# Attention of the first two chunks issued among the later chunks' k, q, v, g products, with buffers of its own

## The chip, the cores and the metric

One core of one Trainium2 chip runs the kernel. The metric is device time in microseconds, the median of several executions. Matrix work is in fp32r with every operand split into a high and a low part, so one product of fp32 quality is three matmuls.

## What is computed

A decoder trunk of two layers over 2048 positions of width 1024, and a last norm. Layer 0 is a gated short convolution. Layer 1 is stick-breaking attention with 8 heads of 64. Cut to what matters here:

```python
h = rmsnorm(x, norm_a)
b, c, xin, g = split(h @ w_in_a, 4)
x = x + ((b * conv3(c * xin)) * silu(g)) @ w_out_a
k, v = split(rmsnorm(x, norm_kv) @ w_kv, 2)
q, g = split(rmsnorm(x, norm_b) @ w_in_b, 2)
...
z = q @ k.T / 8                       # per head, keys before the query only
rev = reverse_cumsum(log_sigmoid(-z))
o = exp(z + rev) @ v
...
x = x + (o * silu(g)) @ w_out_b
return rmsnorm(x, norm_f)
```

## The kernel before, in words

Positions lie reversed along the free axis (a host layout), in four chunks of 512 columns; features lie on the 128 partitions. The two layers' products are made with a fast scheme of seven block products for two chunks at once, chunks (0, 1) and then (2, 3): `fast_unit` (line 848) forms a unit, seven products of 12 matmuls each of 128x128 by 128x512 (84 matmuls), into three PSUM banks named fa, fd and fe. `fast_operands` (742) forms the operands b11, t1, t2, b22, t3, b21, t4 of a pair from its rows, and `operand` (682) gives each a place among the tags that the `HOMES` table names.

The weights of a unit are seven sums and differences of blocks, each split into high and low. `fast_weights` (804) either loads them from DRAM, where an earlier call put them, or loads four raw blocks (`raw_blocks`, 795, which multiplies by the norm's gain on GpSimd), forms the seven on VectorE (`combine`, 781), splits them, uses them, and stores them to DRAM for the next pair. Two of the eight k, q, v, g units are prepared ahead (`prepare_pair`, 845; `READY` is 0 and 4).

After the mixer's output products (`po` parts) come the k and q units (`pair_kq`, 992, parts kq00 to kq03 for chunks 0 and 1, kq20 to kq23 for chunks 2 and 3) and the v and gate units (`pair_vg`, 1002). They store split k (four DMAs of 64 partitions for each pair of heads and chunk), split q, the differences of neighbouring v rows, and silu(g) to DRAM. Each unit forms two chunks, so all of chunks 0 and 1 is in DRAM when the first four units of each sort are done.

`attend` (1030) is the attention of one chunk and one head. It looks only at the query's own 128-block and the one before it; what that leaves over is gathered in a tile `left`, and if any of it isn't zero a full version runs at the end (it isn't entered with these inputs). It loads q2 (two DMAs of 64 partitions), kt and vv, each with two buffers. Eight z matmuls give the logits, ScalarE makes R by a sigmoid, GpSimd masks (`affine_select`), VectorE runs four scans, GpSimd copies `left`; seven or eight transposes (wt) bring the blocks the other way, ScalarE and VectorE split them into wth and wtl, and av matmuls multiply them with vv; two operations put the head's half into the tile ot. `gate_kept` (1240) adds the first v row, multiplies by the gate, both on GpSimd, and splits the result into the og operands. There are 32 heads, parts a00 to a37, and gates g00 to g32.

The output product (`out_kept`, 1256, parts o0 to o2; `out_b_last` and `finish` for chunk 3) takes og and the output weights wob, which `keep_ob` (1234) loads for good into eight tiles of the `act` tag; these tiles are free only when the operands of the products are done with. `fold_gains` (914) has split those weights and put them into DRAM. `norm_kept` (1268) ends chunks 0 to 2.

What sets the order: all operations are recorded first. `PLAN` (36) gives each part a start and an end, a key is laid over the part's operations, and `Recorder.order` (285) picks one operation after another by a list schedule: the one that can start first by its own costs of engines, buffers in turn, and DMA (`DMA_RATE`, 70), and the lower key among equals. The order in which each engine issues is then fixed. An engine does its queue strictly in order, and SyncE (SP) issues all the DMAs of this part, so a load that waits for a buffer holds up all the loads and stores behind it. Buffers of one tag are given in turn.

Every recorded operation is emitted from line 358, so the profile's rows all have that line and are told apart by tile names.

Of the kernel before, what the change touches and what calls it, by code (L numbers as in the profile page):

```python
# [10 lines left out]
F32 = mybir.dt.float32  # L11
F32R = mybir.dt.float32r
# [4 lines left out]
P = 128  # L17
# [10 lines left out]
FIRST = (("act", [2, CH], NA), ("R", [CH], NR), ("q2", [2, CH], 2), ("kt", [CH], 2), ("vv", [CH], 2), ("wth", [CH], NWTS),  # L28
# [41 lines left out]
DMA_RATE, DMA_BEFORE, DMA_AFTER, FLY = 0.36, 1.0, 2.8, 8  # L70
# [296 lines left out]
def kernel(  # L367
# [56 lines left out]
    k_all = [dram.tile([P, S], F32, name=f"k_d_{h}") for h in range(NH)]  # L424
    k_d = [[k_all[h][:, cols(c)] for h in range(NH)] for c in range(NCH)]
# [121 lines left out]
    def norm_x_late(c, between=None):  # L547

        hc, xs = [], []
        for k in range(KD):  # L550
            if between is not None:
                between(k)
            tag, bufs = (("og", KD), ("ld", NL) if k < NL else ("vv", 2) if k == NL else ("ot", 2))[c]
            x = sb.tile([P, CH], F32, name=f"xh_{c}_{k}", tag=tag, bufs=bufs)
            nc.sync.dma_start(out=x, in_=xT[k * P:(k + 1) * P, cols(c)])
            xs.append(x)
            ga = gains["a"][:, k:k + 1]
            hk = act_tile(f"h_{c}", k)
# [123 lines left out]
    def operand(c, nm, k, raw, eng=nc.vector):  # L682

        if k == 0:
            fast_b[c, nm] = []
            other = {"t1": "t4", "t4": "t1"} if isinstance(c, tuple) and c[0] == "kq" else {}
            home[nm] = list(HOMES[other.get(nm, nm)])
        tag = home[nm].pop(0)
        if tag in ("act", "q2"):
            t = sb.tile([P, 2, CH], F32R, name=f"op_{nm}_{c}_{k}", tag=tag, bufs=BUFS[tag])  # L690
            pair = (t[:, 0, :], t[:, 1, :])
        else:
            tags = [tag, home[nm].pop(0)]
# [48 lines left out]
    def fast_operands(key, load, eng, hold=False):  # L742
# [11 lines left out]
        for k in range(Q):  # L754
            b.append(raw("b12", 0, k, *((("ot", 2) if k < 2 else ("p", 2)) if hold else ())))
            eng.tensor_sub(a[k], b[k], a[k])
            operand(key, "t1", k, a[k])
# [7 lines left out]
        for k in range(Q):  # L765
            if not hold:
                b[k] = raw("c12", 0, k, "ot", 2)
            eng.tensor_sub(b[k], d[k], b[k])
# [223 lines left out]
    def pair_kq(c0, i):  # L992
        for c, (k, q) in enumerate(pair_unit(c0, i, f"kq{i}"), c0):
            hl = halves(f"khl_{c}_{i}_", k)
            for j in range(2):
                for m in range(2):
                    nc.sync.dma_start(out=k_d[c][2 * i + j][m * 64:(m + 1) * 64, :], in_=hl[m][j * 64:(j + 1) * 64, :])
# [32 lines left out]
    def attend(c, h, ot):  # L1030
# [3 lines left out]
        q2 = sb.tile([P, 2, CH], F32R, name=f"q2_{nm}", tag="q2", bufs=2)  # L1034
        for i in range(2):
            nc.sync.dma_start(out=q2[i * 64:(i + 1) * 64, :, :].bitcast(F32), in_=q_d[c][hb][hi_ * 64:(hi_ + 1) * 64, :, :])
        kt = sb.tile([P, CH + P], F32R, name=f"kt_{nm}", tag="kt", bufs=2)
        vt = sb.tile([P, 5, 2, 64], F32R, name=f"vv_{nm}", tag="vv", bufs=2)
        n = 5 if c else 4
        at = 4 * (NCH - 1 - c)  # L1040
        nc.sync.dma_start(out=kt[:, 0:n * P].bitcast(F32), in_=k_all[h][:, at * P:(at + n) * P])
# [4 lines left out]
        for i in range(2):  # L1046
# [8 lines left out]
            r = sb.tile([P, CH], F32, name=f"R_{nm}_{i}", tag="R", bufs=NR)  # L1055
# [18 lines left out]
        for i, places in enumerate((((1, 0), (1, 1), (2, 1), (2, 2)), ((3, 2), (3, 3), (0, 0), (4, 3)))):  # L1074
# [6 lines left out]
            wh = sb.tile([P, CH], F32R, name=f"wth_{nm}_{i}", tag="wth", bufs=NWTS)  # L1081
            wl = sb.tile([P, CH], F32R, name=f"wtl_{nm}_{i}", tag="wtl", bufs=NWTS)
# [15 lines left out]
    def attention(c, h, ot):  # L1098
# [4 lines left out]
        for i in range(2):  # L1103
            nc.scalar.dma_start(out=q2[i * 64:(i + 1) * 64, :, :].bitcast(F32), in_=q_d[c][hb][hi_ * 64:(hi_ + 1) * 64, :, :])
# [135 lines left out]
    def gate_kept(c, k, ot):  # L1240
# [3 lines left out]
        nc.gpsimd.tensor_mul(ot, ot, sg)  # L1244
        og = act_tile(f"og_{c}", k)
        og_t.setdefault(c, []).append(og)
        split(og[:, 0, :], og[:, 1, :], ot)
# [123 lines left out]
    part("fl", any_left)  # L1371
    for c in range(3):
# [10 lines left out]
    with tc.If(some != 0, preferred_fallthrough_block=False):  # L1383
        og_t.clear()
        acc_b.clear()
        for c in range(NCH):
            for hb in range(NH // 2):
                ot = sb.tile([P, CH], F32, name=f"all_ot_{c}_{hb}", tag="ot", bufs=2)
# [32 lines left out]
```

## Time and profile before

| | |
|---|---|
| median of 3 runs | 1430.42 us (1422.63 to 1435.01) |
| the profiled execution's own time | 1427.81 us |
| its span, first to last instruction | 1425.8 us |
| mean granted TensorE clock | 0.976 |
| moved by DMA | 409.31 MB, 287 GB/s |
| last product unit's matmuls end | about 1175 us |
| attention's z matmuls | 954.6 to 1343.7 us |
| output products (pob) | 1188.4 to 1392.1 us |

How to read the rows that follow: a row of a stretch gives its bounds, its length, then busy time and number of instructions for PE (matmul), PEld (weight load), DVE (VectorE), ACT (ScalarE) and POOL (GpSimd), then the granted clock, the busy share of the 16 DMA engines and GB/s. A row of a group gives the engine, the operation, out<-in by tile names, the shape and the count, then the busy time and the mean of one in ns, then the idle time of the engine before them and what ended it. A row of the chain gives its start, its length and what it was. Matmuls are pipelined, so the mean of one is longer than the step from one to the next. A row of a DMA gives the count, the size and the median time from issue to landing.

### The profile page before, as it was taken

What the parts mean: (1) busy time and instruction counts of PE and PEld (TensorE: products, weight loads), DVE (VectorE), ACT (ScalarE), POOL (GpSimd) and SP (SyncE); (2) the same over time, 40 slices, a digit from 0 to 9 for tenths busy, and PEclk for the clock granted to TensorE, in tenths of its full rate; (3) what the DMA queues carried; (4) which work ended last, traced back from release to release, by engine and by line L of the source; (5) the groups of instructions that cost most, each with busy time, mean ns of one, the idle gap of its engine ahead of it and who ended that gap; (6) DMA issues with size and microseconds to landing.
All of it is one profiled execution on the core that took longest, in us unless ns stands there. A gap on an engine that the chain in (4) does not pass through costs nothing.

```text
span 1425.8 us, 18966 instructions
## 1 busy us (share of the span) xinstructions
PE 1330.1 (93%) x6174; PEld 1096.2 (77%) x6174; DVE 986.0 (69%) x1557; ACT 578.2 (41%) x999; POOL 389.5 (27%) x447
## 2 busy tenths in 40 slices
PE   7999999999999999999999999998899986787994
PEld 6787888888888888888887787776778775576883
DVE  6999787879867655566584886568632387777864
ACT  6344443335333322233332444443422255455542
POOL 6252000000200001001216532242100135466775
PEclk9999999999999999999999999998999998999996
DMA  9648998688988999979997889995899999988433
GB/s 296 214 149 264 336 322 290 230 284 284 371 320 284 344 381 347 371 271 371 334 361 289 284 264 336 349 379 174 280 319 325 312 300 300 282 242 220 154 128 121
DMA packets 216413, 409.31 MB, mean 287 GB/s; under 512 B 20208, under 2 KB 89840, under 8 KB 216304
## 3 DMA queue, kind: packets, MB, share of 16 engines
q1 hardware_dynamic: 215104, 407.97, 85.4%
q8 instruction: 51, 0.84, 0.2%
q14 instruction: 58, 0.48, 0.1%
q0 software_dynamic: 160, 0.02, 0.1%
q10 hardware_dynamic: 1040, 0.00, 0.0%
HBM read 238.06 MB, written 169.87 MB: 286 GB/s over the span
## 4 chain that ended last, share of the span: by engine, by line
PE 70%; DMA 12%; DVE 11%; issue 3%; ACT 2%; POOL 1%; SPq 0%; DVEq 0%; ACTq 0%; POOLq 0%
PE fa_B L358 11%; PE fa_C L358 10%; PE fa_o L358 6%; PE fd_B L358 5%; PE fd_C L358 5%; PE fa_vg L358 5%; PE fa_kq L358 5%; PE pob L358 4%; DMA kt<-k_d 4%; DMA q<-q_d 3%; PE fd_o L358 3%; PE fe_B L358 3%; PE fe_C L358 2%; PE fd_vg L358 2%; PE fd_kq L358 2%
## 5 line engine op out<-in xcount | busy, mean ns | idle before, releaser
L358 POOL COPY halo<-p 128x2 f32<-128x2 f32 x32 | 17.3, 539 | 395.1 <-DVE p L358 394.6
L358 POOL TENSOR_TENSOR acc_x<-acc_x,sq_x 128x512 f32<-128x512 f32 x52 | 76.0, 1461 | 124.2 <-ACT sq_x L358 123.4
L358 DVE TENSOR_TENSOR_SCAN R<-R,ones 128x256 f32<-128x256 f32 x128 | 97.2, 798 | 7.4 <-POOL R L358 7.3
L358 PE MATMUL pob<-og,wob 128*128 128x512 f32 x360 | 98.6, 407 | 0.2 <-DVE og L358 0.2
L358 PE MATMUL fa_C<-op_t,whl_s_C 128*128 128x512 f32 x336 | 85.5, 390 | 0.6 <-DVE op_t L358 0.6
L358 PE MATMUL fa_B<-op_t,whl_s_B 128*128 128x512 f32 x336 | 83.1, 389 | 0.0
L358 PEld LDWEIGHTS pob<-og,wob 128*128 128x128 f32 x360 | 64.6, 191 | 11.5 <-DVE x L358 0.6
L358 PEld LDWEIGHTS fa_C<-op_t,whl_s_C 128*128 128x128 f32 x336 | 62.7, 188 | 13.9 <-DVE op_t L358 1.0
L358 PEld LDWEIGHTS fa_B<-op_t,whl_s_B 128*128 128x128 f32 x336 | 63.1, 188 | 13.1
L358 PE MATMUL z<-kt,q 128*128 128x256 f32 x256 | 49.4, 326 | 23.7 <-DMA kt<-k_d 21.9
L358 ACT ACTIVATE sq_x<-x 128x512 f32<-128x512 f32 x55 | 34.6, 631 | 77.9 <-DVE x L358 74.8
L358 PEld LDWEIGHTS z<-kt,q 128*128 128x128 f32 x256 | 40.0, 216 | 28.3 <-issue 22.0
L358 PE MATMUL wt<-ident,R 128*128 128x128 f32 x248 | 49.4, 289 | 7.4 <-DVE R L358 5.3
L358 DVE TENSOR_TENSOR wtl<-wt,wth 128x512 fp32r<-128x512 f32 x64 | 41.7, 665 | 19.0 <-ACT wth L358 16.6
L358 DVE SCALAR_TENSOR_TENSOR cv<-p,cw,cv 128x512 f32<-128x512 f32 x64 | 49.6, 775 | 6.8 <-ACT cv L358 3.5
L358 ACT CAST wth<-wt 128x512 fp32r<-128x512 f32 x64 | 35.9, 574 | 41.1 <-PE wt L358 33.3
L358 POOL TENSOR_SCALAR_AFFINE_SELECT R<-R 128x256 f32<-128x256 f32 x64 | 36.5, 578 | 58.4 <-ACT R L358 57.8
L358 PE MATMUL av<-wth,vv 128*128 128x256 f32 (+1 forms) x152 | 39.6, 293 | 11.5 <-DMA vv<-v_d 6.0
L358 DVE TENSOR_TENSOR x<-x,fa_o 128x512 f32<-128x512 f32 x32 | 21.9, 686 | 38.9 <-PE fa_o L358 28.4
L358 ACT ACTIVATE R<-z 128x512 f32<-128x512 f32 x64 | 36.9, 601 | 26.2 <-PE z L358 25.8
L358 PE MATMUL fa_B<-op_t,whl_a_B 128*128 128x512 f32 x168 | 45.4, 390 | 0.0
L358 PE MATMUL fa_C<-op_b,whl_a_C 128*128 128x512 f32 x168 | 45.3, 390 | 0.0
(1012 smaller groups left out, 3709.1 us busy)
## 6 DMA issues: line engine op xcount, KB each, us to landing
sw_s_C<-whl_s_C SPq DMA_DIRECT2D x32, 512.0 KB, 3.9
sw_s_B<-whl_s_B SPq DMA_DIRECT2D x32, 512.0 KB, 4.3
whl_s_o<-sw_s_o SPq DMA_DIRECT2D x32, 512.0 KB, 5.7
q<-q_d SPq DMA_DIRECT2D x64, 256.0 KB, 7.9
sw_a_C<-whl_a_C SPq DMA_DIRECT2D x24, 512.0 KB, 4.2
sw_a_B<-whl_a_B SPq DMA_DIRECT2D x24, 512.0 KB, 3.6
whl_s_C<-sw_s_C SPq DMA_DIRECT2D x24, 512.0 KB, 5.5
whl_s_B<-sw_s_B SPq DMA_DIRECT2D x24, 512.0 KB, 6.0
```

The lines of the kernel that those rows point to most:

```text
L358: getattr(o.engine.engine, o.name)(*map(real, o.args), **{k: real(v) for k, v in o.kw.items()})
```

## The change

- The keys of the plan from xk0 on are new, those of po22, po23 and fold too: fold comes earlier, and the heads of chunks 0 and 1 (a00 to a17) lie among kq2 and vg2. `DMA_RATE` goes from 0.36 to 0.33.
- The heads of chunks 0 and 1 get other places: kta and vva, new tags of one buffer each, for kt and vv; q2 takes a tile of the weights' tag whl (8 buffers), R one of og (8), wth and wtl of acc (2). The tag ot (2 buffers) goes; what used it takes kta and vva.
- The gated outputs of chunks 0 and 1 go to DRAM and are loaded and split later, in new parts h0 and h1 (`load_og`).
- q2 is loaded by one DMA over 128 partitions, which repeats each source row, so two neighbouring partitions hold the same row; k is stored with its high and low part on alternate partitions, by two DMAs of 128 partitions for a pair of heads in place of four of 64.
- The weights of a k, q, v or g unit that wasn't prepared ahead are formed from the raw blocks for each pair of chunks. They are no longer stored to DRAM or loaded back; for the later pair their sums and differences run on GpSimd.
- In the k, q, v, g units the operands t1, t2 and t4 trade places: t1 gets the tiles of q2, kt and vv, t2 those of R, wth and wtl, t4 those of act.

```diff
+    "kq20": (938.809, 984.97), "vg20": (994.417, 1022.11),
+    "kq21": (1117.4, 1118.71), "vg21": (1025.39, 1044.52), "kq22": (1066.01, 1107.98), "vg22": (1121.85, 1133.59),
+    "kq23": (1121, 1126.72), "vg23": (1045.19, 1089.24), "wo": (1165.87, 1206.27), "a00": (967.407, 970.474),
...
-    k_all = [dram.tile([P, S], F32, name=f"k_d_{h}") for h in range(NH)]
+    k_all = [dram.tile([2 * P, S], F32, name=f"k_d_{i}") for i in range(NH // 2)]
...
-            other = {"t1": "t4", "t4": "t1"} if isinstance(c, tuple) and c[0] == "kq" else {}
+            other = {"t1": "t4", "t2": "t1", "t4": "t2"} if isinstance(c, tuple) and c[0] == "kq" else {}
...
     def fast_weights(c, nm, key, srcs=None, gain=None):
         w = {}
+        if gain is not None and key not in split_d:
+            def put(n, raw):
+                w[n] = w_tile(f"{n}_{nm}")
+                split(w[n][:, 0], w[n][:, 1], raw)
+
+            combine(raw_blocks(nm, srcs, gain), put, nc.gpsimd if c == ("kq", 2) else nc.vector)
+            return w
...
-            for j in range(2):
-                for m in range(2):
-                    nc.sync.dma_start(out=k_d[c][2 * i + j][m * 64:(m + 1) * 64, :], in_=hl[m][j * 64:(j + 1) * 64, :])
+            for m in range(2):
+                nc.sync.dma_start(out=k_all[i][m::2, cols(c)], in_=hl[m])
...
-        q2 = sb.tile([P, 2, CH], F32R, name=f"q2_{nm}", tag="q2", bufs=2)
-        for i in range(2):
-            nc.sync.dma_start(out=q2[i * 64:(i + 1) * 64, :, :].bitcast(F32), in_=q_d[c][hb][hi_ * 64:(hi_ + 1) * 64, :, :])
-        kt = sb.tile([P, CH + P], F32R, name=f"kt_{nm}", tag="kt", bufs=2)
-        vt = sb.tile([P, 5, 2, 64], F32R, name=f"vv_{nm}", tag="vv", bufs=2)
+        early = c < 2
+        qtag, ktag, vtag, rtag, wtags = (("whl", NWB), ("kta", 1), ("vva", 1), ("og", KD), (("acc", 2), ("acc", 2))) if early else (
+            ("q2", 2), ("kt", 2), ("vv", 2), ("R", NR), (("wth", NWTS), ("wtl", NWTS)))
...
+        q2 = sb.tile([P, 2, CH], F32R, name=f"q2_{nm}", **home(qtag))
+        nc.sync.dma_start(out=q2.bitcast(F32), in_=q_d[c][hb][hi_ * 64:(hi_ + 1) * 64].unsqueeze(1).to_broadcast([64, 2, 2, CH]))
+        kt = sb.tile([P, CH + P], F32R, name=f"kt_{nm}", **home(ktag))
+        vt = sb.tile([P, 5, 2, 64], F32R, name=f"vv_{nm}", **home(vtag))
...
         nc.gpsimd.tensor_mul(ot, ot, sg)
+        if c < 2:
+            nc.sync.dma_start(out=og_d[c][k], in_=ot)
+        else:
+            split_og(c, k, ot)
...
+    def load_og(c):
+        for k in range(4):
+            r = ld512(f"ogl_{c}_{k}")
+            nc.sync.dma_start(out=r, in_=og_d[c][k])
+            split_og(c, k, r)
...
+    for c in range(2):
+        part(f"h{c}", load_og, c)
```

More of the change, by code (lines that the diff above doesn't have):

```diff
@@ L27 @@
 READY = (0, 4)
-FIRST = (("act", [2, CH], NA), ("R", [CH], NR), ("q2", [2, CH], 2), ("kt", [CH], 2), ("vv", [CH], 2), ("wth", [CH], NWTS),
+FIRST = (("act", [2, CH], NA), ("R", [CH], NR), ("q2", [2, CH], 2), ("kt", [CH], 2), ("vv", [CH], 2), ("kta", [CH + P], 1), ("vva", [CH + P], 1), ("wth", [CH], NWTS),
          ("wtl", [CH], NWTS), ("wraw", [Q, P], NRAW), ("whl", [2, Q, P], NWB))
@@ L68 @@
 SEM = 0.11
-DMA_RATE, DMA_BEFORE, DMA_AFTER, FLY = 0.36, 1.0, 2.8, 8
+DMA_RATE, DMA_BEFORE, DMA_AFTER, FLY = 0.33, 1.0, 2.8, 8
 class Base:
@@ L423 @@
     x1_d = [[dram.tile([P, CH], F32, name=f"x1_d_{c}_{k}") for k in range(KD)] for c in range(NCH)]
-    k_all = [dram.tile([P, S], F32, name=f"k_d_{h}") for h in range(NH)]
-    k_d = [[k_all[h][:, cols(c)] for h in range(NH)] for c in range(NCH)]
+    k_all = [dram.tile([2 * P, S], F32, name=f"k_d_{i}") for i in range(NH // 2)]
+    k_d = [[k_all[h // 2][(h % 2) * P:(h % 2 + 1) * P, cols(c)] for h in range(NH)] for c in range(NCH)]
     q_d = [[dram.tile([P, 2, CH], F32, name=f"q_d_{c}_{h}") for h in range(NH // 2)] for c in range(NCH)]
@@ L552, in norm_x_late @@
                 between(k)
-            tag, bufs = (("og", KD), ("ld", NL) if k < NL else ("vv", 2) if k == NL else ("ot", 2))[c]
+            tag, bufs = (("og", KD), ("ld", NL) if k < NL else (("vv", 2), ("kta", 1), ("vva", 1))[k - NL])[c]
             x = sb.tile([P, CH], F32, name=f"xh_{c}_{k}", tag=tag, bufs=bufs)
@@ L754, in fast_operands @@
         for k in range(Q):
-            b.append(raw("b12", 0, k, *((("ot", 2) if k < 2 else ("p", 2)) if hold else ())))
+            b.append(raw("b12", 0, k, *((("kta", 1), ("vva", 1), ("p", 2), ("p", 2))[k] if hold else ())))
             eng.tensor_sub(a[k], b[k], a[k])
@@ L766, in fast_operands @@
             if not hold:
-                b[k] = raw("c12", 0, k, "ot", 2)
+                b[k] = raw("c12", 0, k, ("kta", "vva")[k % 2], 1)
             eng.tensor_sub(b[k], d[k], b[k])
@@ L1033, in attend, with home @@
         nm = f"{c}_{h}"
-        q2 = sb.tile([P, 2, CH], F32R, name=f"q2_{nm}", tag="q2", bufs=2)
-        for i in range(2):
-            nc.sync.dma_start(out=q2[i * 64:(i + 1) * 64, :, :].bitcast(F32), in_=q_d[c][hb][hi_ * 64:(hi_ + 1) * 64, :, :])
-        kt = sb.tile([P, CH + P], F32R, name=f"kt_{nm}", tag="kt", bufs=2)
-        vt = sb.tile([P, 5, 2, 64], F32R, name=f"vv_{nm}", tag="vv", bufs=2)
+        early = c < 2
+        qtag, ktag, vtag, rtag, wtags = (("whl", NWB), ("kta", 1), ("vva", 1), ("og", KD), (("acc", 2), ("acc", 2))) if early else (
+            ("q2", 2), ("kt", 2), ("vv", 2), ("R", NR), (("wth", NWTS), ("wtl", NWTS)))
+        def home(tag):
+            return {"tag": tag[0], "bufs": tag[1]}
+        q2 = sb.tile([P, 2, CH], F32R, name=f"q2_{nm}", **home(qtag))
+        nc.sync.dma_start(out=q2.bitcast(F32), in_=q_d[c][hb][hi_ * 64:(hi_ + 1) * 64].unsqueeze(1).to_broadcast([64, 2, 2, CH]))
+        kt = sb.tile([P, CH + P], F32R, name=f"kt_{nm}", **home(ktag))
+        vt = sb.tile([P, 5, 2, 64], F32R, name=f"vv_{nm}", **home(vtag))
         n = 5 if c else 4
         at = 4 * (NCH - 1 - c)
-        nc.sync.dma_start(out=kt[:, 0:n * P].bitcast(F32), in_=k_all[h][:, at * P:(at + n) * P])
+        nc.sync.dma_start(out=kt[:, 0:n * P].bitcast(F32), in_=k_all[hb][hi_ * P:(hi_ + 1) * P, at * P:(at + n) * P])
         nc.sync.dma_start(out=vt[:, 0:n].bitcast(F32), in_=v_all[h][:, at:at + n])
@@ L1054, in attend @@
                         nc.ops[-1].deps.add(nc.ops[-2])
[L1055 removed]
+            r = sb.tile([P, CH], F32, name=f"R_{nm}_{i}", **home(rtag))
             nc.scalar.activation(r, ps, AF.Sigmoid, scale=-0.125)
@@ L1080, in attend @@
                 nc.tensor.transpose(wt[:, j * P:(j + 1) * P], blk(kb, qi), ident)
-            wh = sb.tile([P, CH], F32R, name=f"wth_{nm}_{i}", tag="wth", bufs=NWTS)
-            wl = sb.tile([P, CH], F32R, name=f"wtl_{nm}_{i}", tag="wtl", bufs=NWTS)
+            wh = sb.tile([P, CH], F32R, name=f"wth_{nm}_{i}", **home(wtags[0]))
+            wl = sb.tile([P, CH], F32R, name=f"wtl_{nm}_{i}", **home(wtags[1]))
             split(wh[:, 0:n], wl[:, 0:n], wt[:, 0:n])
@@ L1102, in attention @@
         q2 = sb.tile([P, 2, CH], F32R, name=f"q2_{nm0}", tag="q2", bufs=2)
-        for i in range(2):
-            nc.scalar.dma_start(out=q2[i * 64:(i + 1) * 64, :, :].bitcast(F32), in_=q_d[c][hb][hi_ * 64:(hi_ + 1) * 64, :, :])
+        nc.scalar.dma_start(out=q2.bitcast(F32), in_=q_d[c][hb][hi_ * 64:(hi_ + 1) * 64].unsqueeze(1).to_broadcast([64, 2, 2, CH]))
         av = psum.tile([P, CH], F32, name=f"av_{nm0}", tag="av", bufs=NAV)
@@ L1244, in gate_kept, with split_og @@
         nc.gpsimd.tensor_mul(ot, ot, sg)
+        if c < 2:
+            nc.sync.dma_start(out=og_d[c][k], in_=ot)
+        else:
+            split_og(c, k, ot)
+    def split_og(c, k, r):
         og = act_tile(f"og_{c}", k)
         og_t.setdefault(c, []).append(og)
-        split(og[:, 0, :], og[:, 1, :], ot)
+        split(og[:, 0, :], og[:, 1, :], r)
+    def load_og(c):
[3 more added lines that the diff above has]
+            split_og(c, k, r)
     def x2_rows(c):
@@ L1387 @@
             for hb in range(NH // 2):
-                ot = sb.tile([P, CH], F32, name=f"all_ot_{c}_{hb}", tag="ot", bufs=2)
+                ot = sb.tile([P, CH], F32, name=f"all_ot_{c}_{hb}", tag="og", bufs=KD)
                 for h in (2 * hb, 2 * hb + 1):
```

53 rows, old and new, of the table PLAN are left out of this document.

## Prediction

> **What bounds the kernel now.** I read the page first, then the busy times of five stretches of the span, the chain that ended last, and the matmuls in order of time where one head of the attention already runs among products.
>
> ```profile
> span 1425.8 us, 18966 instructions
> ...
> PE 1330.1 (93%) x6174; PEld 1096.2 (77%) x6174; DVE 986.0 (69%) x1557; ACT 578.2 (41%) x999; POOL 389.5 (27%) x447
> ...
> GB/s 296 214 149 264 336 322 290 230 284 284 371 320 284 344 381 347 371 271 371 334 361 289 284 264 336 349 379 174 280 319 325 312 300 300 282 242 220 154 128 121
> ```
>
> TensorE is the bound of the whole: busy 93% of the span. What a stage loses is read from stretches: 790 to 1143 us are the k, q, v, g products, 1143 to 1312 most of the attention, 1312 to 1398 the rest of it with the output products, then the last norm.
>
> ```profile
> 790.00:960.00 170.00, 165.15 (x742) 134.07 (x740) 121.55 (x189) 77.81 (x138) 61.09 (x54) 1.00 0.95 327
> 960.00:1143.00 183.00, 168.79 (x747) 136.15 (x747) 87.90 (x125) 56.27 (x98) 23.26 (x37) 0.97 0.85 283
> 1143.00:1312.00 169.00, 128.12 (x787) 109.85 (x788) 130.22 (x209) 89.28 (x162) 87.00 (x137) 0.91 0.97 268
> 1312.00:1398.00 86.00, 84.33 (x444) 70.26 (x442) 68.56 (x112) 44.56 (x75) 65.90 (x62) 0.99 0.47 154
> 1398.00:1426.00 28.00, 7.04 (x32) 6.61 (x32) 9.29 (x20) 3.68 (x7) 10.05 (x8) 0.58 0.30 107
> 1143.00:1250.00 107.00, 79.46 (x479) 67.87 (x480) 83.70 (x129) 54.77 (x101) 47.97 (x84) 0.89 1.04 295
> ```
>
> The columns are PE, PEld, DVE, ACT, POOL busy with counts, granted clock, DMA share, GB/s. In the third row PE is idle 41 of 169 us, the clock falls to 0.91 and the DMA engines are busy 0.97 of the time (1.04 up to 1250 us, at only 295 GB/s; the page has slices at 371 and 379). The chain there is loads behind loads:
>
> ```profile
> 565.98 2.72 PE fa_C L358 x12
> ...
> 1206.99 10.22 DMA kt<-k_d
> 1218.57 9.09 DMA q<-q_d
> 1227.67 8.82 DMA q<-q_d
> 1236.51 9.73 DMA q<-q_d
> ```
>
> So the attention stage is set by its loads, all on SP's queue, and not by PE; in the product stage the same chain is PE alone, 12 matmuls in 2.72 us (0.227 each).
>
> **How much is lost.** The counts and the price of a small matmul:
>
> ```profile
> L358 PE MATMUL pob<-og,wob 128*128 128x512 f32 x360 | 98.6, 407 | 0.2 <-DVE og L358 0.2
> ...
> L358 PE MATMUL z<-kt,q 128*128 128x256 f32 x256 | 49.4, 326 | 23.7 <-DMA kt<-k_d 21.9
> ...
> L358 PE MATMUL wt<-ident,R 128*128 128x128 f32 x248 | 49.4, 289 | 7.4 <-DVE R L358 5.3
> ...
> L358 PE MATMUL av<-wth,vv 128*128 128x256 f32 (+1 forms) x152 | 39.6, 293 | 11.5 <-DMA vv<-v_d 6.0
> ```
>
> ```profile
> 954.63 1.12 PE L358 MATMUL z<-kt,q 128*128 128x256 f32 x8
> 955.58 0.63 PE L358 MATMUL fa_vg<-op_t_('kq', 0)_2_7452,whl_s_vg 128*128 128x512 f32 x2
> ...
> 976.47 0.28 PE L358 MATMUL av<-wth,vv 128*128 128x256 f32 x1
> ...
> 983.22 0.27 PE L358 MATMUL av<-wtl,vv 128*128 128x128 f32 x1
> ```
>
> Eight z take 0.95 us among products (954.63 to the next start), 0.12 each; I price all attention matmuls at that. From 790 to 1398 the four rows hold 2720 matmuls: 1344 of the products (16 units of 84, by the code) and 384 of the output (360 pob and, by the code, 24 in the last step) at 0.227 make 392 us; 808 of the attention (256 + 248 + 2 x 152) at 0.12 make 97; the other 184, short ones and the last mixer-output products, at an estimated 0.14, 26. That is 515 us of work in 608: 93 are lost. The third stretch holds some 617 attention matmuls, 110 of the output and 60 others (its 787, split by names): 74 + 25 + 12 = 111, so 58 are lost there. The fourth loses about 3. The other 32 are lost in the first two (353 us, 9%), of which 19 show as idle (4.9 + 14.2); the first alone idles 2.9%. The 28 us after 1398 stay.
>
> **The change, part by part.**
>
> Attention of chunks 0 and 1 (16 of 32 heads) goes among the later products. PE's work is the same; 16 heads are 48 us by the price above. What is left for the last stage is 16 heads (48), 384 output matmuls (87) and about 5 of sums: 140 us; the product part becomes 515 - 140 = 375. The product part's rate of loss has its ends in today's product rows: 2.9% (idle of 790 to 960, where weights are formed from raw as the later pair's now will be) and 9% (all of 790 to 1143). I take the middle, 6%: 375/0.94 = 399, 24 lost. For the last stage the ends are the fourth stretch (3 of 86, 3.5%) and the third (58 of 169, 34%). Half of the heads, spread over as much output work, are nearer to the fourth: I take 7%, 140/0.93 = 150.5, 10.5 lost. Together 34.5 in place of 93: **58.5 us less**.
>
> Loads, stores and SP's queue. Each head loads q, kt and vv:
>
> ```profile
> q<-q_d SPq DMA_DIRECT2D x64, 256.0 KB, 7.9
> ...
> kt<-k_d SPq DMA_DIRECT2D x24, 320.0 KB, 7.8
> vv<-v_d SPq DMA_DIRECT2D x24, 320.0 KB, 7.2
> ...
> sw_s_kq<-whl_s_kq SPq DMA_DIRECT2D x12, 512.0 KB, 5.1
> sw_s_vg<-whl_s_vg SPq DMA_DIRECT2D x12, 512.0 KB, 6.6
> ```
>
> 1.18 MB a head, 18.9 MB for 16, enter the product part. Out of it go the weight stores of six units (12 + 12 of these two rows and 18 more by the code, 42 of 0.52 MB, 22 MB) and 42 loads, for which 24 raw loads of 0.26 MB come: 15.7 MB less. 107 MB in 353 us now (327 x 170 + 283 x 183) become 107 + 19 - 38 + 6 (the fold of w_out_b, planned earlier) + 4 (gated outputs to DRAM and back) = 98 in 399: 246 GB/s, under all these rows. The last stage moves 18.9 + 4.2 (wob) + 8.4 (x) + 8 (out) + 2 = 42 MB in 150 us, 280 GB/s, which is no longer far below the 295 of the saturated row. q in one issue in place of two, and k stores halved, take 64 issues off SP.
>
> Single buffers. kta and vva have one buffer, so the next vva load waits on SP for the last av of the head before. Behind it in SP's queue stand raw weights and k, q, v stores, for which the product units wait. Today's one interleaved head spends 976.47 to 983.2 in av; with 7.2 to land, a head then takes at least 14 us, 16 heads 227. The first v is in DRAM at about 900 us (an estimate from the product order), the product part ends at 790 + 399 = 1189: 289 us, 18 a head. It fits with 4 us to spare, so I price it at nothing; the rival below is the other end.
>
> Weights formed anew: for six units of the later pair 42 casts on ACT, 42 subtractions on DVE, and on POOL 24 gains and 24 sums.
>
> ```profile
> L358 DVE TENSOR_TENSOR fr_a_vg<-fr_a_vg,fr_a_vg 128x512 f32<-128x512 f32 x12 | 10.3, 858 | 0.1
> ...
> L358 DVE TENSOR_TENSOR whl_s_kq<-fr_a_kq,whl_s_kq 128x512 fp32r<-128x512 f32 x12 | 9.8, 821 | 2.3 <-ACT whl_s_kq L358 2.3
> ...
> L358 DVE TENSOR_TENSOR fr_a_kq<-fr_a_kq,fr_a_kq 128x512 f32<-128x512 f32 x12 | 8.2, 686 | 0.0
> ...
> L358 ACT CAST whl_s_kq<-fr_a_kq 128x512 fp32r<-128x512 f32 x12 | 7.5, 624 | 10.3 <-DVE fr_a_kq L358 3.4 <-PE fa_kq L358 2.4 <-PE fd_kq L358 1.8
> ...
> L358 POOL TENSOR_TENSOR fr_a_kq<-fr_a_kq,g_kv 128x512 f32<-128x512 f32 x6 | 7.1, 1191 | 35.9 <-DMA fr_a_kq<-in_w_kv_dram 35.9
> ```
>
> ACT 42 x 0.62 = 26 us, DVE 42 x 0.82 = 34, POOL 24 x 1.19 = 29 and 24 sums, whose nearest POOL row is this one with two whole inputs:
>
> ```profile
> L358 POOL TENSOR_TENSOR acc_x<-acc_x,sq_x 128x512 f32<-128x512 f32 x52 | 76.0, 1461 | 124.2 <-ACT sq_x L358 123.4
> ...
> L358 DVE TENSOR_TENSOR_SCAN R<-R,ones 128x256 f32<-128x256 f32 x128 | 97.2, 798 | 7.4 <-POOL R L358 7.3
> ...
> L358 DVE TENSOR_TENSOR wtl<-wt,wth 128x512 fp32r<-128x512 f32 x64 | 41.7, 665 | 19.0 <-ACT wth L358 16.6
> ```
>
> 24 x 1.46 = 35. DVE also gets 16 heads of four scans, two wtl and one ot (0.68): 5.2 us, 83. So DVE in the product part is 121.6 + 87.9 + 34 + 83 = 327 of 399 us, 82%. Its first stretch now has 121.55 of 170, 71%, beside a PE that idles 2.9%. All this lies beside PE's 375; without that cover it would be a bound of its own, the second rival. POOL is at 84 + 64 + about 31 (selects, left) + about 20 (gates) = 199 of 399, not a bound.
>
> The gated outputs of chunks 0 and 1 go to DRAM and back (8 stores, 8 loads, 8 splits later): off the path while they are back before the wob loads have landed. Other homes of the operands t1, t2, t4 only choose what frees first at the end of the products; bounds 0 to 3 us either way, in the 7%.
>
> Sum: 1427.8 (this execution's own time, 2 us over its span) - 58.5 = 1369. The median, 1430.42, is 2.6 higher, inside the runs' spread of 12.
>
> **Rivals.**
>
> 1. Loads still pace the last stage: 42 MB at the third row's 268 GB/s are 157 us, and the 4.2 MB of wob stand before its first output product, 14 at 295: 171, 20 more, **1389**. For it: that row's share of 0.97. Against: half of the heads.
> 2. POOL holds DVE up. If each of the 48 new POOL operations (64 us) delays a DVE operation by its length, DVE has 391 of 399; at 93% use the part takes 420, 21 more, **1390**. For it: the same subtraction and sum on DVE take 686 to 858. Against: 0.17 us of growth is far from 1.2. The Trainium skill, SBUF — State Buffer, "Who interferes with whom", says that "a DVE instruction with two SBUF inputs contends with a GpSimd instruction that reads SBUF"; by that rule this rival would hold, and the row's growth agrees in sign, not in size.
> 3. The loads of a head come faster: q as one load over 128 partitions rather than two over 64 lets the last stage move at the 371 of the page's better slices (42 MB in 113 us, so PE alone sets it), and losses are the low ends, 11 + 5: **1351**, lower still if the product part idles less than today. The Trainium skill, same page, "Door 1: The DMA port swizzle", says that 64 partitions reach only half of the ports; no row here shows one load alone.
> 4. The other side: the single buffers make heads nearly serial. From its first z to its last av the interleaved head takes 28.6 us (954.6 to 983.2); if kt can't be loaded under the head before, a period is 7.8 + 14 and some 2 of queueing, 24 us: 384 in a room of 289, and PE, in order, stands before a late z, 95 us: **1464**. It decides from 18 us a head; at 21.7 nothing is gained, at 22.8 it is slower by 1%. For it: today, with two buffers, z waits 21.9 us on kt. Against: kta is free after eight z, long before av.
> 5. The order puts the heads behind the products after all, so that the same loads stand at the end: **1425**. Against: the plan's numbers for chunks 0 and 1 lie among those of kq2 and vg2.
>
> **Chances.** 0.55 for the forecast (1350 to 1390), 0.1 each for rivals 1, 2 and 3, 0.08 for 4, 0.07 for 5. A measurement of this kernel can tell about 1% from no change (under 1416, over 1445). Faster 0.86, the same 0.07, slower 0.07. The range takes in rivals 1 to 3, product losses of 9% and a last stage at 20% (35): gain 21, 1407; below, rival 3 with 15 to spare: 1336 to 1408.
>
> **What would show it.** Right: z and av from about 910 us on; under 10 us of PE idle per 170 us until the products end near 1190; the stretch from there to the last output matmul 150 us, with the clock above 0.95; DMA share under 0.9 before 1190; no sw_s_kq or sw_s_vg stores. Wrong: PE waiting on kta or vva more than 4 us a head, DVE above 90% there, or a last stage over 170 us.

## The result and the profile after

| | before | after |
|---|---|---|
| median in the runs side by side | 1432.2 us (1422.63 to 1435.01) | 1383.73 us (1383.31 to 1384.27) |
| ratio | | 0.9673, 95% interval 0.9627 to 0.972 |
| the profiled execution's own time | 1427.81 us | 1383.76 us |
| last matmul of the mixer's output products (fa_o) starts | 805.5 us | 826.4 us |
| last matmul of the product units (fe_vg) starts | 1174.9 us | 1202.2 us |
| last output matmul (pol) starts | 1397.5 us | 1354.2 us |

The change is faster by 3.3%. The time lies inside the predicted range (1336 to 1408) and 14.7 us above the point forecast of 1369. First the head of the page after: span, busy times of the engines, traffic.

```profile
span 1381.8 us, 18877 instructions
...
PE 1321.8 (96%) x6174; PEld 1085.6 (79%) x6174; DVE 1028.7 (74%) x1599; ACT 596.3 (43%) x1041; POOL 450.4 (33%) x495
...
DMA packets 218268, 375.74 MB, mean 272 GB/s; under 512 B 18480, under 2 KB 100400, under 8 KB 218160
```

As many matmuls as before, 44 us less span, and 33.6 MB less traffic (409.31 before). The stretches of after, with the columns of the stretches in the prediction: two in the mixer, three in the product part, then what comes behind it, split in two.

```profile
300.00:350.00 50.00, 43.49 (x185) 35.30 (x184) 43.31 (x71) 23.82 (x42) 2.83 (x4) 0.93 0.80 276
650.00:820.00 170.00, 162.57 (x702) 130.94 (x701) 113.61 (x182) 55.69 (x95) 54.92 (x39) 0.98 0.95 335
820.00:960.00 140.00, 139.23 (x647) 114.95 (x646) 111.44 (x180) 68.80 (x123) 40.68 (x45) 1.00 0.69 233
960.00:1045.00 85.00, 79.81 (x387) 64.65 (x387) 80.39 (x105) 46.76 (x84) 45.77 (x52) 1.00 0.76 260
1045.00:1180.00 135.00, 134.36 (x701) 110.99 (x699) 109.89 (x147) 68.67 (x125) 90.29 (x103) 1.00 0.69 222
1180.00:1300.00 120.00, 113.99 (x670) 96.80 (x669) 97.46 (x156) 71.55 (x126) 76.70 (x96) 0.97 0.90 309
1300.00:1354.00 54.00, 53.19 (x279) 43.03 (x278) 40.95 (x80) 25.43 (x44) 43.54 (x42) 1.00 0.45 151
```

From 820 to 1180 us PE idles 6.6 us in 360 and the DMA engines are busy 0.69 to 0.76 of the time; before, the attention stretch alone idled 41 of 169 at 0.97. What follows, 1180 to 1354, idles 6.8 of 174. The first two rows are the other side. The same stretches in the kernel before, the second one up to the end of its mixer:

```profile
300.00:350.00 50.00, 50.00 (x222) 41.11 (x220) 44.93 (x73) 23.94 (x41) 1.55 (x4) 1.00 0.85 278
650.00:805.00 155.00, 151.77 (x672) 124.75 (x671) 94.93 (x158) 49.67 (x85) 53.06 (x39) 0.99 0.93 333
```

So something was lost before the products begin, for which the prediction's sum has no term. The longest waits of PE in the whole span of after (the longest, 6.7 us at the kernel's start, is as before and is left out), and the place of the first of them in the order of time, on PE and on DVE:

```profile
PE fa_B L359 <- DVE whl_s_B L359: 6.0, 1, 6.0
PE pst_x L359 <- DVE acc_x L359: 3.4, 1, 3.4
PE fa_o L359 <- ACT op_t_('o', 2)_2_6683 L359: 3.2, 1, 3.2
```

```profile
340.00 3.94 PE L359 MATMUL fa_B<-op_t,whl_s_B 128*128 128x512 f32 x10 [5.96 <-DVE whl_s_B L359]
```

```profile
333.05 0.70 DVE L359 TENSOR_TENSOR whl_s_B<-fr_a_B,whl_s_B 128x512 fp32r<-128x512 f32 x1
333.65 0.69 DVE L359 TENSOR_TENSOR xc<-xb,xc 128x512 f32<-128x512 f32 x1
334.25 0.70 DVE L359 TENSOR_TENSOR xb<-xb,xb 128x512 f32<-128x512 f32 x1
334.85 2.08 DVE L359 SCALAR_TENSOR_TENSOR xb<-xb,g_a,rs 128x512 f32<-128x512 f32 x3
336.84 0.70 DVE L359 TENSOR_TENSOR xc<-xb,xc 128x512 f32<-128x512 f32 x1
337.44 1.90 DVE L359 TENSOR_TENSOR xb<-xb,xb 128x512 f32<-128x512 f32 x3
339.25 0.70 DVE L359 TENSOR_TENSOR whl_s_B<-fr_a_B,whl_s_B 128x512 fp32r<-128x512 f32 x1
```

DVE never stands still there. Between two splits of weights it works through nine operations on xb and xc, and the matmul that needs the second split waits 5.96 us. This is an order, not a slow instruction. And the matmuls of a head, with the landings of its loads (count, KB each, median us):

```profile
L359 PE MATMUL z<-kt,q 128*128 128x256 f32 x256 | 44.3, 289 | 0.0
...
L359 PE MATMUL av<-wth,vv 128*128 128x256 f32 x96 | 27.0, 292 | 0.4 <-DVE ot L359 0.4
```

```profile
q<-q_d SPq DMA_DIRECT2D x32, 512.0 KB, 5.6
...
kt<-k_d SPq DMA_DIRECT2D x24, 320.0 KB, 5.7
vv<-v_d SPq DMA_DIRECT2D x24, 320.0 KB, 5.0
```

The 21.9 us that z waited for kt and the 6.0 that av waited for vv are gone altogether. kt lands in 5.7 us where it took 7.8, and q brings twice the bytes in 5.6 where it took 7.9.

### The profile page after: what moved, and what is told of

Same layout as the page of the kernel before. It is cut to its first block, busy times and chain, and to the rows that moved or that the text cites. A ratio compares the mean times of both kernels' runs of the same rounds, so it can differ in the third digit from the quotient of the medians.

```text
span 1381.8 us, 18877 instructions
## 1 busy us (share of the span) xinstructions
PE 1321.8 (96%) x6174; PEld 1085.6 (79%) x6174; DVE 1028.7 (74%) x1599; ACT 596.3 (43%) x1041; POOL 450.4 (33%) x495
## 2 busy tenths in 40 slices
DMA packets 218268, 375.74 MB, mean 272 GB/s; under 512 B 18480, under 2 KB 100400, under 8 KB 218160
## 4 chain that ended last, share of the span: by engine, by line
PE 75%; DVE 13%; POOL 4%; issue 4%; DMA 2%; ACT 2%; SPq 0%; DVEq 0%; POOLq 0%; ACTq 0%
PE fa_B L359 11%; PE fa_C L359 10%; PE fd_B L359 5%; PE fd_C L359 5%; PE fa_kq L359 5%; PE fa_vg L359 5%; PE fa_o L359 4%; PE pob L359 4%; PE fd_vg L359 3%; PE fd_kq L359 3%; PE fe_C L359 3%; PE fe_B L359 2%; PE fd_o L359 2%; PE av L359 1%; DVE R L359 1%
## 5 line engine op out<-in xcount | busy, mean ns | idle before, releaser
L359 ACT ACTIVATE sq_x<-x 128x512 f32<-128x512 f32 x55 | 34.5, 633 | 70.1 <-DVE x L359 52.2
L359 ACT ACTIVATE cv<-p,cw 128x512 f32<-128x512 f32 x32 | 23.1, 724 | 70.1 <-DVE p L359 66.7
L359 PE MATMUL z<-kt,q 128*128 128x256 f32 x256 | 44.3, 289 | 0.0
L359 PE MATMUL fe_C<-op_b,whl_a_C 128*128 128x512 f32 x168 | 43.5, 394 | 0.4 <-DVE op_b L359 0.4
L359 PEld LDWEIGHTS wt<-ident,R 128*128 128x128 f32 x248 | 32.1, 143 | 13.8 <-DVE R L359 3.0
L359 PE MATMUL fd_C<-op_t,whl_s_C 128*128 128x512 f32 x168 | 42.6, 390 | 0.2 <-DVE whl_s_C L359 0.2
```

Of the source, the lines that this page charges most:

```text
L359: getattr(o.engine.engine, o.name)(*map(real, o.args), **{k: real(v) for k, v in o.kw.items()})
```

## The experiments

Three things might have made the 48 us: the move of the heads, the weights formed anew, and the new loads of q (with the stores of k). A fourth thing, the planner's rate, touches only the order. The way of the gated outputs through DRAM, the new homes and the new keys of the products were not run by themselves. Times are medians, with the ratio to runs of the kernel before, taken beside them, and its 95% interval.

**The rate alone.** The theory is that 0.33 reorders the mixer; the rival is that the mixer was pushed by what the rest of the change does. The kernel before with one number changed:

```diff
-DMA_RATE, DMA_BEFORE, DMA_AFTER, FLY = 0.36, 1.0, 2.8, 8
+DMA_RATE, DMA_BEFORE, DMA_AFTER, FLY = 0.33, 1.0, 2.8, 8
```

> The kernel before with one number of the order's cost model changed, the DMA rate, 0.33 in place of 0.36. Theory A (the rate alone reorders the mixer, and that order is slower there): the last mixer-output matmul moves from 805 us to about 826, the stretch 300 to 350 us loses some 8 us of TensorE, and the time is 1440 to 1460. Theory B (the mixer's loss came with the new buffer tags and keys): the mixer ends at 803 to 808 as before, and the time is 1425 to 1437.

1453.91 us, ratio 1.0164 (1.011 to 1.0218): 23 us slower. Its row of 300 to 350 us:

```profile
300.00:350.00 50.00, 43.49 (x184) 35.26 (x183) 43.36 (x70) 23.83 (x42) 2.84 (x4) 0.93 0.79 274
```

It is the row of after to the hundredth of PE's busy time. The last fa_B starts at 654.8 us (641.8 before, 654.4 after) and the last fa_o at 832.6. The rate alone brings the mixer's loss.

**The rate only where the change needs it.** The change, with the mixer's parts planned at 0.36 and what follows at 0.33; and the change with 0.36 throughout:

```diff
-DMA_RATE, DMA_BEFORE, DMA_AFTER, FLY = 0.33, 1.0, 2.8, 8
+DMA_RATE, DMA_BEFORE, DMA_AFTER, FLY = (0.36, 0.33), 1.0, 2.8, 8
+MIXER = ("m", "x0", "x1", "x2", "s", "w0", "w1", "w2", "w3", "w4", "w8", "ox", "po", "y")
...
-                pipe = max(pipe, o.fin + DMA_BEFORE) + o.bytes / DMA_RATE * 1e-6
+                pipe = max(pipe, o.fin + DMA_BEFORE) + o.bytes / DMA_RATE[not o.part.startswith(MIXER)] * 1e-6
```

> The changed kernel with the old rate 0.36 for the parts up to the mixer's output and 0.33 behind them. Theory A: the mixer is again as before, its last output matmul near 805 to 810, the rest as in the changed kernel, 1363 us (1357 to 1370). Theory B: no gain, 1380 to 1388.

> The changed kernel with the DMA rate 0.36 throughout, the mixer's order as before. Theory A (the rate's cost is in the mixer alone): 1362 to 1378, like the kernel with the rate split (1373). If 0.33 is what makes the order of the attention fit the chip: 1380 to 1400, with TensorE waiting on kt or vv.

1373.36 us, ratio 0.9588 (0.9541 to 0.9635), and 1374.7, ratio 0.9609 (0.9574 to 0.9644). Both beat the change and the kernel before; the first lies between its two theories. In it the last fa_o starts at 803.3, 23 us sooner than in the change, but only 10 of them reach the end: behind the mixer the first heads now come at 919.5 rather than 943.7, and the stretch of 960 to 1045 us does less (369 matmuls, where the change does 387) at a clock of 0.92 instead of 1.00.

```profile
960.00:1045.00 85.00, 78.95 (x369) 62.94 (x368) 68.42 (x105) 43.15 (x78) 32.59 (x51) 0.92 0.74 239
```

Where the rest of the 13 us goes was not followed; the keys are those of the change, and new ones for this earlier start were not tried.

**Without the move.** The change with the heads of chunks 0 and 1 behind the products, with their double buffers and keys of before; weights anew, transfers of q and k and gated outputs by way of DRAM stay:

```diff
-        early = c < 2
+        early = False
...
-    "a00": (967.407, 970.474),
+    "a00": (1161.9, 1177.3),
...
```

> The changed kernel with everything but the move: the heads of chunks 0 and 1 have the keys of the kernel before, behind the products, and the double buffers; weights formed anew, q in one load, k in two stores and the late split of the gated outputs stay. Theory A (the move is where the time comes from): 1425 us (1412 to 1440), with TensorE idle 35 us or more between the products' end and the last output product. Theory C (the lighter loads and stores are the gain): 1384 to 1400.

1433.26 us, ratio 1.0012 (0.9991 to 1.0034): the whole gain is gone. From 1143 to 1312 us PE is busy 141.48 of 169, at a granted clock of 0.88:

```profile
1143.00:1250.00 107.00, 83.88 (x452) 70.20 (x450) 80.30 (x126) 51.03 (x92) 49.79 (x93) 0.81 0.92 318
1143.00:1312.00 169.00, 141.48 (x795) 118.72 (x794) 137.88 (x210) 88.39 (x159) 88.52 (x146) 0.88 0.85 288
```

In the whole kernel z waits for kt only 0.6 us. PE waits for DVE and ACT instead, within a head (wt for R 11.4 us, wt and av for wtl 9.7). So here, where the loads are quick, PE in heads that stand alone waits for their own chain of scans and splits, and has no other work to put between.

**Without the weights formed anew.** The change, with the weights of the first pair stored and loaded again for the second, as the kernel before does:

```diff
-        if gain is not None and key not in split_d:
-            def put(n, raw):
-                w[n] = w_tile(f"{n}_{nm}")
-                split(w[n][:, 0], w[n][:, 1], raw)
-
-            combine(raw_blocks(nm, srcs, gain), put, nc.gpsimd if c == ("kq", 2) else nc.vector)
-            return w
```

> The changed kernel, but the weights of the k, q, v, g units are stored and loaded back for the later pair as before. Theory A: the DMA engines have room among the products, so 1382 to 1395. Theory C (less weight traffic is part of the gain): 1400 to 1425, with the DMA share near 1 until 1180 us and loads of kt and vv that land in 7 us or more.

1424.47 us, ratio 0.9957 (0.9931 to 0.9982). Without it the rest of the change is worth next to nothing. Its product part, in the same three stretches as after:

```profile
820.00:960.00 140.00, 132.51 (x607) 107.23 (x606) 100.93 (x163) 64.12 (x114) 38.31 (x43) 1.00 0.93 321
960.00:1045.00 85.00, 73.91 (x310) 57.88 (x310) 71.19 (x95) 39.36 (x70) 34.16 (x34) 0.91 0.85 302
1045.00:1180.00 135.00, 133.23 (x697) 110.49 (x696) 74.38 (x115) 51.84 (x94) 35.71 (x67) 0.99 0.94 322
```

The DMA engines are 0.85 to 0.94 busy at 302 to 322 GB/s, where the change has 0.69 to 0.76 at 222 to 260. PE falls behind up to 1045 us: 917 matmuls from 820 on, where the change does 1034. The last product matmul starts at 1223.9 instead of 1202.2, and from there to the last output matmul it takes 173 us instead of 152. With the heads' loads and the weights' stores and loads in one part, the products themselves run late. Theory C has the time and the busy DMA engines, but not its other sign: from 820 to 1180 us kt and vv (320 KB) land in 5.3 and 6.3 us (4.8 and 5.2 in the change), not in 7 or more. PE waits there for splits of weights, 12 us from 820 to 1250, and for no load of a head. Whether the traffic makes those splits late, or SyncE's queue, or the weight tiles that a store keeps occupied, was not separated.

**The transfers of q and k alone.** Rival 3 had given them a price. The kernel before at its own rate, with only these edits of the change:

```diff
-            for j in range(2):
-                for m in range(2):
-                    nc.sync.dma_start(out=k_d[c][2 * i + j][m * 64:(m + 1) * 64, :], in_=hl[m][j * 64:(j + 1) * 64, :])
+            for m in range(2):
+                nc.sync.dma_start(out=k_all[i][m::2, cols(c)], in_=hl[m])
...
-        for i in range(2):
-            nc.sync.dma_start(out=q2[i * 64:(i + 1) * 64, :, :].bitcast(F32), in_=q_d[c][hb][hi_ * 64:(hi_ + 1) * 64, :, :])
+        nc.sync.dma_start(out=q2.bitcast(F32), in_=q_d[c][hb][hi_ * 64:(hi_ + 1) * 64].unsqueeze(1).to_broadcast([64, 2, 2, CH]))
```

> The kernel before with only the transfers of q and k changed: q of a head in one load over 128 partitions, k in two stores. Theory A (two parts, the move and the lighter weight traffic, make the gain, each needing the other): 1415 to 1432, the attention still behind the products. Theory R3 (rival 3 of the prediction: loads over 128 partitions come faster): 1390 to 1410, with q, kt and vv landing in 6 us or less between 1143 and 1312 us and over 340 GB/s there.

1406.29 us, ratio 0.9831 (0.9794 to 0.9868), 24 us without any move, in the range of theory R3. The attention stretch, to be read against the prediction's rows of 1143 to 1250 (79.46 busy, 479 matmuls, 295 GB/s) and 1143 to 1312:

```profile
1143.00:1250.00 107.00, 91.63 (x586) 80.21 (x585) 99.56 (x154) 66.90 (x122) 63.96 (x101) 0.94 0.96 340
1143.00:1312.00 169.00, 149.70 (x936) 130.63 (x935) 150.99 (x238) 106.51 (x190) 115.16 (x161) 0.95 0.86 301
```

The landings in that stretch, of the kernel before and then of this one (the count is that of the window):

```profile
q<-q_d SPq DMA_DIRECT2D x50, 256.0 KB, 8.0
kt<-k_d SPq DMA_DIRECT2D x20, 320.0 KB, 8.3
vv<-v_d SPq DMA_DIRECT2D x18, 320.0 KB, 8.0
```

```profile
q<-q_d SPq DMA_DIRECT2D x27, 512.0 KB, 5.6
kt<-k_d SPq DMA_DIRECT2D x22, 320.0 KB, 6.1
vv<-v_d SPq DMA_DIRECT2D x20, 320.0 KB, 5.0
```

kt and vv were loaded in the same way in both, and they land 2.2 and 3.0 us sooner.

The same with the change's rate, so that the later steps can be counted from one base:

> The same with the DMA rate 0.33, so with the changed kernel's mixer order: the corner of a square of four whose other corners are 1433 (weights formed anew, heads late), 1424 (weights stored, heads moved) and 1384 (both). If the two parts simply added, this corner would be 1433 + 1424 - 1384 = 1473; if each did nothing without the other, 1433 or less. Theory A (they need each other): 1430 to 1450.

1432.38 us, ratio 1.0018 (1.0001 to 1.0035): the rate's 23 us and the transfers' 22 to 24 cancel.

**What it is in these transfers.** First the load of q of the change with k stored in four DMAs of 64 partitions; then q in two loads of 256 KB, as many and as large as before, but over 128 partitions each. Both diffs are against the kernel with both edits (1406):

```diff
-            for m in range(2):
-                nc.sync.dma_start(out=k_all[i][m::2, cols(c)], in_=hl[m])
+            for j in range(2):
+                for m in range(2):
+                    nc.sync.dma_start(out=k_all[i][j * P + m:(j + 1) * P:2, cols(c)], in_=hl[m][j * 64:(j + 1) * 64, :])
```

> The kernel before at its own rate (0.36), with q in one load over 128 partitions as the change has it, and k stored in four transfers of 64 partitions as the kernel before has it. The pair of edits together took 24 us off (1406). Theory Q (the load of q is what did it: 64-partition loads slowed all loads around them): 1403 to 1412, z's wait on kt stays near 5 us. Theory S (the fewer stores of k did it): 1420 to 1430, z's wait on kt back toward 22 us.

```diff
-        nc.sync.dma_start(out=q2.bitcast(F32), in_=q_d[c][hb][hi_ * 64:(hi_ + 1) * 64].unsqueeze(1).to_broadcast([64, 2, 2, CH]))
+        for m in range(2):
+            nc.sync.dma_start(out=q2[:, m, :].bitcast(F32),
+                              in_=q_d[c][hb][hi_ * 64:(hi_ + 1) * 64, m, :].unsqueeze(1).to_broadcast([64, 2, CH]))
```

> The kernel before at its own rate (0.36), with q in two loads of 256 KB as the kernel before has them in number and size, but each over 128 partitions (half of the columns each) instead of 64; k stored in two transfers as the change has it. Theory of the partitions (a load over 64 partitions is slow and slows the others): 1400 to 1412, q and kt landing in 5 to 6 us. Theory of the issues (half as many issues on SyncE's queue did it): 1422 to 1432, landings near 8 us.

1397.12 us, ratio 0.9782 (0.9758 to 0.9806), and 1391.65, ratio 0.9742 (0.9718 to 0.9765). Both are faster than their theories allowed. Neither the fewer stores nor the fewer issues are needed for the gain. With two loads over 128 partitions, the landings and the stretch:

```profile
q<-q_d SPq DMA_DIRECT2D x52, 256.0 KB, 4.9
vv<-v_d SPq DMA_DIRECT2D x21, 320.0 KB, 5.1
kt<-k_d SPq DMA_DIRECT2D x21, 320.0 KB, 5.6
```

```profile
1143.00:1250.00 107.00, 92.52 (x594) 79.64 (x593) 100.86 (x156) 66.53 (x122) 66.67 (x104) 0.95 0.98 340
```

In this stretch 256 KB over 128 partitions land in 4.9 us, 256 KB over 64 in 8.0. All three kernels do alike in the stretch (91.63, 92.34 and 92.52 us busy of 107). Why their ends differ by up to 15 us is not settled: the planner gives each a somewhat different order of the products ahead.

**The later pair's sums on VectorE**, for rival 2:

```diff
-            combine(raw_blocks(nm, srcs, gain), put, nc.gpsimd if c == ("kq", 2) else nc.vector)
+            combine(raw_blocks(nm, srcs, gain), put, nc.vector)
```

> The changed kernel with the later pair's 24 weight sums on VectorE in place of GpSimd. Rival 2 (GpSimd holds VectorE up by the length of its operations): faster by 5 to 20 us. Otherwise VectorE, busy 78 to 95% from 960 to 1180 us, has 24 x 0.7 = 17 us more to do: 1384 to 1400.

1389.0 us, ratio 0.9715 (0.9679 to 0.9751), not faster than the change. The weights' subtractions on DVE get shorter in the mean, 842 ns in the change and 758 here:

```profile
L359 DVE TENSOR_TENSOR whl_s_kq<-fr_a_kq,whl_s_kq 128x512 fp32r<-128x512 f32 x24 | 20.1, 842 | 0.1
```

```profile
L359 DVE TENSOR_TENSOR whl_s_kq<-fr_a_kq,whl_s_kq 128x512 fp32r<-128x512 f32 x24 | 18.0, 758 | 0.7 <-ACT whl_s_kq L359 0.5
```

The kernel before, which has no such sums on GpSimd, shows 821 in the prediction's row. These means hide what happens to a single operation. Two of DVE in the change, and two sums on GpSimd beside them:

```profile
1091.30 0.69 DVE L359 TENSOR_TENSOR wtl<-wt,wth 128x512 fp32r<-128x512 f32 x1 [0.44 <-ACT wth L359]
1093.11 1.78 DVE L359 TENSOR_TENSOR whl_s_kq<-fr_a_kq,whl_s_kq 128x512 fp32r<-128x512 f32 x1
```

```profile
1090.22 1.79 POOL L359 TENSOR_TENSOR fr_a_kq<-fr_a_kq,fr_a_kq 128x512 f32<-128x512 f32 x1
1092.76 1.58 POOL L359 TENSOR_TENSOR fr_a_kq<-fr_a_kq,fr_a_kq 128x512 f32<-128x512 f32 x1 [0.75 <-ACT whl_s_kq L359]
```

The second DVE operation has both inputs in SBUF, starts while a sum runs, and ends 0.55 us after it; the first takes wt from PSUM and keeps its 0.69 us. So it is throughout: from 820 to 1202 us DVE has 234 sums, differences and products of 128x512 with both inputs in SBUF, and 52 of them start under a sum, difference or product on GpSimd. These have a median of 1.46 us, and 48 of them end 0.52 to 0.58 us after GpSimd's; the other 182 have a median of 0.69. Together the waiting is 35 us of DVE time, against 22 in the kernel before (790 to 1143 us), and the 24 sums stand for 8 of it, since only ten operations ran into one. PE waits for no weights of these units. So rival 2's mechanism is there, up to 1.1 us an operation, but the sums cost DVE 8 us by it, where on DVE they would be 17 us of work.

**Two last variants on top of the split rate** (1373.36): q in two loads over 128 partitions, by the diff shown above; and q in two loads over 64, as before, with k as the change stores it. In the second the rows of q and k don't line up, so other rows are multiplied; its loads and its instructions are those meant.

> The change with its rate split (0.36 for the mixer's parts, 0.33 behind them; 1373 so far), and q in two loads of 256 KB, each over 128 partitions. In the kernel before, those two loads (1392) came out 14 us better than one of 512 KB (1406), with z waiting 0.4 us on kt instead of 4.7. Theory that the shorter load brings the first half of a head sooner wherever heads are: 1360 to 1370. Theory that it helps only where the heads stand close together at the end, and the change has spread them, so that z there no longer waits at all (0.0 in the change): 1370 to 1378.

> The change with its rate split (1373 so far), but q in two loads over 64 partitions as the kernel before has them; k in its two stores. The move and the weights formed anew are all there. Theory that the loads of q stand for some 22 us wherever heads are (they slow their neighbours): 1388 to 1400. Theory that the move spreads the heads so far that slow loads are hidden: 1372 to 1380, the gain is then the move's alone and the two edits are two ways to the same 40 us.

1383.69 us, ratio 0.969 (0.9666 to 0.9713), and 1382.28, ratio 0.9687 (0.9664 to 0.9711). These two were timed in another set of runs than the split rate; by the ratios, each to the kernel before beside it, they are 14 to 15 us behind it, where the medians say 10 and 9. The first fell outside both expectations: shorter loads of q, and slower. Its product part is like that of the split rate, and behind it wt waits for the scans:

```profile
L360 PE MATMUL wt<-ident,R 128*128 128x128 f32 x248 | 50.2, 281 | 10.4 <-DVE R L360 5.2 <-DVE t_x L360 2.3 <-DVE wtl L360 2.0
```

With the split rate that wait is 2.5 us, and z, which waits for nothing there, waits 2.3 us for kt here. The planner's order of PE's work differs from about 916 us on; that this is the cause was not isolated. The second lies between its two theories: with the move in place, loads of q over 64 partitions cost 9 to 14 us, where the new transfers were worth 22 to 24 in the kernel before. z waits 6.4 us in it, 5.2 of them on nothing that the profile shows. The loads themselves are as slow as ever (from 1180 to 1354 us; with the split rate q 5.8, vv 4.5, kt 6.1):

```profile
q<-q_d SPq DMA_DIRECT2D x26, 256.0 KB, 8.1
vv<-v_d SPq DMA_DIRECT2D x16, 320.0 KB, 6.6
kt<-k_d SPq DMA_DIRECT2D x14, 320.0 KB, 7.7
```

So the move hides part of what the new loads remove, and the two share part of one gain.

## Why the prediction was right, and where not

**The account, from the runs at one rate.** With the transfers of q and k new and the rate at 0.33:

| | weights stored and loaded | weights formed anew |
|---|---|---|
| heads behind the products | 1432.4 | 1433.3 |
| heads among the products | 1424.5 | 1383.7 |

Weights alone: nothing. Move alone: 8 us. Both: 48 to 49. Some 40 us come from the pair together. Where the weights are formed anew, 38 MB of traffic leave the part that the heads' loads enter (the change moves 375.74 MB in all, and 413.49 with the weights stored). That this is the reason is argued from the two DMA shares and not isolated, as said above. The corner at 1432.4 is also without the change's keys of the products, its new homes and the way of the gated outputs through DRAM, which the corner at 1433.3 has, so "weights alone" takes these in. Counted from the kernel before: the rate +23, the transfers -22, move and weights -48. The terms don't simply add: in the change the rate costs 9 us (1374.7 at 0.36). Each of these kernels has its planner's order, and orders alone moved a time by 10 to 23 us above, so single terms are good to about that; the 40 are more than any of these, but no better known.

**The step that failed** is the assumption in the sum that nothing changes before 790 us: it set "this execution's own time" minus 58.5, and no term for the mixer. The change moves `DMA_RATE` for the whole plan, and the list schedule then orders the mixer's DVE work differently. The last fa_o starts 20.9 us later (826.4 against 805.5), and the rate alone did that, and more, in the first experiment (832.6). From there to the end the profiled execution takes 557.4 us (1383.76 - 826.4), against 622.3 before: 64.9 less, where 58.5 were forecast. 20.9 - 64.9 = -44.0 is the measured difference of the two profiled executions. So, by place in the trace, the miss of 15 us is 21 for the unpriced mixer, less 6 by which the rest did better. By effect it is less: with the mixer planned at the old rate 10 us came back (1373.4, 4 over the forecast), and what the other 4 are stays open. The section on the change lists the new rate; the prediction has no term for it.

**The steps of the sum.**

- Attention among the products: right. 18 heads begin before the last product matmul, the first at 943.7 (about 910 was said, and the mixer is 21 late). By the prices of the prediction the 2681 matmuls from 820 to 1354 are 509 us of work (1727 large ones at 0.227, 808 of the attention at 0.12, 146 others at 0.14), so 25 of 534 us are lost, against the 34.5 forecast.
- The last stage: from 1202.2 to 1354.2 are 152 us, against 150.5, at a clock of 0.97 from 1180 to 1300 and 1.00 behind. Rival 1, loads pacing it at 171, did not occur: the DMA share is 0.90 from 1180 to 1300, but PE waits for no load of a head.
- Traffic and DVE in the product part: 246 GB/s and 82% were forecast ("under all these rows" holds for the two product rows, 327 and 283, not for the last two). From 820 to 1180 they are 235 and 302 of 360 us, 84%:

```profile
820.00:1180.00 360.00, 353.40 (x1733) 290.59 (x1731) 301.72 (x430) 184.23 (x332) 176.75 (x200) 1.00 0.71 235
```

- Single buffers, "it fits with 4 us to spare": right. No wait of PE on kt or vv is in the list, so rival 4 did not occur. Between 1000 and 1147 us the heads start 8 to 22 us apart, most of them about 10. From 820 to 1180 us kt and vv land in 4.8 and 5.2 us rather than the 7.8 and 7.2 of the kernel before (7.2 was put in), so there was more room than the forecast had.
- Weights formed anew were argued as cost, to be hidden; that part was right. The saved traffic was worked out, but used only to show that the DMA engines stay under their limit. The square shows that without the new weights the move gains 8 us and not 49: they were the condition of the gain, and the prediction gave that no rival of its own.
- "q in one issue in place of two" was priced by SP's issues, at nothing. That price was wrong and rival 3's reason was right in kind: 22 to 36 us in the kernel before, with one load or two. Rival 3's result (1351) did not come; with the heads spread, quick loads of q save 9 to 14 us.
- Rival 2, GpSimd holding DVE up: its mechanism is in the trace, its price is not. It let 48 operations delay DVE by 64 us; the waiting grew by 13 (35 against 22), and DVE at 84% stayed beside PE.
- Rival 5, heads behind the products after all: refuted by the z rows, and its price (1425) was near what such a kernel takes at this rate (1433).

Two rules were weighed. The Trainium skill, SBUF — State Buffer, "Door 1: The DMA port swizzle", says that the partitions 0 to 63 reach only 8 of the 16 ports, and 64 to 127 the other 8: the runs agree in direction, 8.0 us over 64 partitions against 4.9 over 128 for the same 256 KB. The Trainium skill, same page, "Who interferes with whom", says that a DVE instruction with two SBUF inputs contends with a GpSimd instruction that reads SBUF. The trace agrees, 1.46 us under a GpSimd operation against 0.69 without. The prediction's "in sign, not in size" was read from the mean of the row at 858 ns, in which ten operations took 0.68 or 0.69 us and two 1.64 and 1.79.

## What to carry to other kernels

Before a stage is moved under another, look at what the other stage spends of the resource that the moved one needs: here the move paid only when the weights were no longer stored and loaded (38 MB less) in the same part. When a planner orders everything, one number changed for the end of a kernel also reorders its beginning, so compare the first part of the two traces before believing a sum for the last. And look at the partitions of a slow load before hiding it: spreading q over 128 partitions, with k's rows stored to match, gave half and more of this change's gain without the move. Where two engines share work, look at single operations: a mean of 0.84 us was made of 0.69 and of up to 1.79.

## What was not expected of the hardware

A load over 64 partitions also delays loads over 128 that are under way beside it. When only q's load changed and k was stored as before, kt went from 8.3 to 5.6 us and vv from 8.0 to 4.2 (1143 to 1312 us), and the traffic from 1143 to 1250 us from 295 to 326 GB/s, while the DMA engines' busy share fell from 1.04 to 0.93. A high busy share in the page thus did not mean that the engines moved all they could. Whether the other loads share the slow ones' engines or stand behind them in the queue was not separated.

A PE that is starved in short gaps was granted a lower clock here: with the heads alone the stretch of 1143 to 1250 us had 0.81, where the change's product part, busy 353 of 360 us, had 1.00. The busy share alone doesn't settle it: in that stretch PE was busy 83.88 of 107 us at 0.81, and in the kernel before 79.46 at 0.89. What else bears on it was not tried.
